# Operand loads of the output projection moved from SyncE's queue to ScalarE's, and the transposes of a token block pinned behind the next block's products

## The chip, the cores and the metric

One NeuronCore of a Trainium2 chip runs one program. The metric is the device time of one execution in microseconds (us). The engines of the core are TensorE (PE in the profile, with its weight loads as PEld), VectorE (DVE), ScalarE (ACT), GpSimd (POOL) and SyncE (SP). Each engine takes its instructions in order and waits at the head of its queue until what the instruction needs is there. A DMA is issued by an instruction in such a queue, too: by SP or by ACT here.

## The reference

Two layers of a decoder trunk over 1024 tokens of width 1024. A layer normalizes its input, projects it, runs several branches (attention of different kinds, in layer 0 a short convolution as well), gates and concatenates them to y, and adds an output projection to the residual stream:

```python
def even_layer(h, mem, layer, norm_g, w_in, w_out, ...):
    u = rms_norm(h, norm_g)
    proj = u @ w_in
    ...
    ya = differential_attention(aq, ak, av, a_qn, a_kn, a_lam, a_on, lam_init)
    yb = short_gated_conv(bh, bc, bb, b_cw, b_cb)
    yx = memory_cross_attention(xq, mem, mem_g, w_mem_kv, x_qn, x_kn)
    y = jnp.concatenate([ya * jax.nn.silu(az), yb * jax.nn.silu(bz), yx * jax.nn.silu(xz)], axis=-1)
    return h + y @ w_out

def rms_norm(x, g):
    xf = x.astype(jnp.float32)
    y = xf * lax.rsqrt(jnp.mean(xf * xf, axis=-1, keepdims=True) + EPS)
    return (y * g.astype(jnp.float32)).astype(x.dtype)
```

The odd layer ends in the same way (forgetting attention and memory attention, no convolution). y has 2048 features in both layers. The first 1024 of them in layer 0 come from differential attention, whose output is normalized per head and token; the kernel applies that factor late, as told below.

## The kernel before

Matrix products in float32 are made of three products of split operands: every operand is written as a high part (a rounded copy, made by ACT, L128) and a low part (the rest, a subtraction on DVE or POOL, L129). `split` (L125) does both.

**The output projection** (`out_proj`, L759, once per layer) multiplies y (tokens by 2048) with a weight of 2048 by 1024. y lies in DRAM, features by tokens (`y_dr`). The 1024 output columns are done in two halves. Half 0 (L773) takes the tokens in pairs of blocks of 128 and fetches and splits the second half's weights meanwhile. Half 1 (L784) takes the eight token blocks one by one, and carries the next layer's entry with it in layer 0: when a block is complete, DVE adds the residual into `hb` (L792), SP stores it (L793), `norm_rows` (L131) normalizes it (ACT's Square, two small steps on POOL, L120 and L122, and `xn` on DVE, L137), and `turn_rows` (L139) transposes `xn` on PE (eight transposes of 128 by 128, L146) and splits the result into the operands `u` of layer 1. The transposes of a block are called as `turn` in the next block's round (L791); those of the last block are kept as `turn_last` and called in layer 1's first projection unit, behind its token block 2 (L205).

`out_blocks` (L728) does the products of a block. For each quarter j of the features it loads a tile yr of 128 by 512 (L739, 256 KB, five buffers). In layer 0 and for j below 2 it also loads the norm factor rn, spread over the partitions (L742, 256 KB, four buffers), and POOL multiplies yr by it (L743). yr is split into yh2 (ACT) and yl2 (DVE), three buffers each, and 12 products follow (L750 to L752). Then the residual's tile rs is loaded (L755). In half 1 of layer 0 the left half of a block, stored before, is loaded back into hb (L788).

**What sets the order.** The kernel is written in a tile framework that schedules every engine's instructions by priorities and by dependencies; the order on an engine is fixed when it is built. All loads and stores stand in SP's queue in this kernel. A load into a buffer waits for the last reader of what was in it: a yr for the DVE split of the yr five tiles before, an rn for POOL's L743 of four tiles before, yh2 and yl2 for PE's products of three tiles before.

Of the kernel before, what the change touches and what calls it, by code (L numbers as in the profile page):

```python
# [15 lines left out]
P = 128  # L16
T = 1024
D = 1024
KC = D // P
# [14 lines left out]
class Trunk:  # L34
# [152 lines left out]
    def token_unit(self, weights, lhs_hi, lhs_lo, nblk, post, together=False):  # L187

        nc = self.nc
# [3 lines left out]
        for t0 in range(0, nblk, step):  # L193
            blks = [(tb, self.bank("pd", "ds"[tb % 2] if together or self.boot else "d"), lhs_hi(tb), lhs_lo(tb)) for tb in range(t0, t0 + step)]
            for k in range(KC):
                h, l = wh[k], wl[k]
                for tb, ps, ah, al in blks:
                    nc.tensor.matmul(ps[:, :n], lhsT=ah(k), rhs=h, start=(k == 0), stop=False)  # L198
                    nc.tensor.matmul(ps[:, :n], lhsT=ah(k), rhs=l, start=False, stop=False)  # L199
                    nc.tensor.matmul(ps[:, :n], lhsT=al(k), rhs=h, start=False, stop=(k == KC - 1))  # L200
            for tb, ps, _, _ in blks:
                with self.tc.high_priority(PRIO_EVAC):
                    post(tb, ps)
            if self.turn_last is not None and t0 == 2:
                self.turn_last()  # L205
                self.turn_last = None
            self.tick()
# [520 lines left out]
    def out_blocks(self, layer, tbs, half, tiles, res, pool, fetch=None):  # L728
# [4 lines left out]
        for j in range(4):  # L733
            if fetch is not None:
                fetch(range(4 * j, 4 * j + 4))
            for tb, ps in zip(tbs, pss):
                ts = slice(tb * P, (tb + 1) * P)
                yr = pool.tile([P, 4, P], F32, name="yr2", tag="yr", bufs=5)
                nc.sync.dma_start(out=yr, in_=self.y_dr[layer][j * 512:(j + 1) * 512, ts].rearrange("(c p) t -> p c t", p=P))  # L739
                if layer == 0 and j < 2:  # L740
                    rn = pool.tile([P, 4, P], F32, name="rn", tag="rn", bufs=4)
                    nc.sync.dma_start(out=rn, in_=self.on_dr[4 * j:4 * j + 4, ts].unsqueeze(0).broadcast_to([P, 4, P]))  # L742
                    nc.gpsimd.tensor_tensor(out=yr, in0=yr, in1=rn, op=ALU.mult)  # L743
# [3 lines left out]
                for i in range(4):  # L747
# [3 lines left out]
                    nc.tensor.matmul(ps, lhsT=yh[:, i, :], rhs=l, start=False, stop=False)  # L751
                    nc.tensor.matmul(ps, lhsT=yl[:, i, :], rhs=h, start=False, stop=(c == 15))  # L752
        for tb, ps in zip(tbs, pss):
# [5 lines left out]
    def out_proj(self, layer, w, res, dst, g_next):  # L759
        nc, tc = self.nc, self.tc  # L760
        with tc.tile_pool(name=f"p2_{layer}", bufs=1, reuse_waits="tile") as p2:
# [22 lines left out]
            for tb in range(NB):  # L784
# [5 lines left out]
                if turn is not None:  # L790
                    turn()  # L791
                nc.vector.tensor_tensor(out=hb[:, 512:], in0=ps, in1=rs, op=ALU.add)  # L792
# [92 lines left out]
```

## Time and profile before

| | us |
|---|---|
| median of 3 runs | 2289.31 (2287.74 to 2291.7) |
| profiled execution | 2293.37 |
| its span in the profile | 2291.6 |
| PE busy in the span | 2198.5 (96%) |
| ACT busy | 1060.1 (46%) |
| layer 0's output projection, about | 950 to 1183 |
| of this, half 1 | 1051 to 1183 |
| layer 1's output projection, about | 2108 to 2290 |

The profiled execution lies 1.8 us above its span, and 4.1 above the median of the runs. A time on the trace's axis counts from the start of the span. In a timeline row an entry such as "x2" means two instructions put together, with the time from the first one's start to the last one's end or the sum of their durations, and the part in brackets is the engine's idle time before it, with what released it.

### The profile page before, as it was taken

To read this page: it belongs to the slowest core of one execution; us is meant where nothing else is said; L and a number is where in the kernel's file an instruction comes from. 1 tells how busy PE (TensorE), PEld (TensorE's weight loads), DVE (VectorE), ACT (ScalarE), POOL (GpSimd) and SP (SyncE) were. 2 spreads that over 40 slices of the span, in tenths; PEclk is the share of its full clock that TensorE was granted. 3 is DMA by queue.
4 is the path that set the end of the run, shared out by engine and by line. 5 is a ranking of instruction groups with operands and counts; after the bars stand their busy time and mean duration, and the time that the engine had idled before them with its cause. 6 is when DMAs were issued, how large, how long until landed. Compare 5 with 4: busy or idle time off the path is not lost.

```text
span 2291.6 us, 35847 instructions
## 1 busy us (share of the span) xinstructions
PE 2198.5 (96%) x12528; PEld 1983.2 (87%) x12528; DVE 1241.3 (54%) x2860; ACT 1060.1 (46%) x2503; POOL 1023.6 (45%) x1356
## 2 busy tenths in 40 slices
PE   7999999999999999797889999999999999998999
PEld 7889989889889899575678999999999999996887
DVE  5646756656656665542334555555555555656332
ACT  5656455555465464421234444444444444545221
POOL 4665555555555552331135555445555555522000
PEclk9999999999999999799999999999999999999999
DMA  5450110210210221665632221121222221215543
GB/s 159 133 148 22 56 55 23 63 55 17 69 46 24 74 70 48 200 196 133 156 104 50 56 55 40 37 51 44 56 54 56 56 61 42 63 49 167 164 148 95
DMA packets 266077, 183.07 MB, mean 80 GB/s; under 512 B 24572, under 2 KB 242844, under 8 KB 265896
## 3 DMA queue, kind: packets, MB, share of 16 engines
q1 hardware_dynamic: 265896, 180.77, 27.9%
q8 instruction: 99, 1.62, 0.3%
q14 instruction: 82, 0.67, 0.1%
HBM read 153.32 MB, written 27.38 MB: 79 GB/s over the span
## 4 chain that ended last, share of the span: by engine, by line
PE 45%; DMA 4%; POOL 2%; DVE 1%; issue 1%; ACT 1%; SPq 0%; POOLq 0%; DVEq 0%; ACTq 0%
PE pd L198 6%; PE pd L200 6%; PE pd L199 6%; PE pss L390 4%; PE pd L750 3%; PE pd L752 3%; PE pd L751 3%; DMA yr<-y_dr 3%; PE pd L230 2%; PE pd L231 2%; PE pd L232 2%; PE pt L424 2%; PE po L438 1%; PE po L437 1%; PE po L436 1%; PE pt L279 1%
## 5 line engine op out<-in xcount | busy, mean ns | idle before, releaser
L198 PE MATMUL pd<-wqh,u 128*128 128x384 f32 (+2 forms) x1536 | 515.1, 337 | 0.6 <-ACT u L128 0.6
L199 PE MATMUL pd<-wql,u 128*128 128x384 f32 (+2 forms) x1536 | 514.1, 335 | 0.0
L200 PE MATMUL pd<-wqh,u 128*128 128x384 f32 (+2 forms) x1536 | 513.1, 334 | 0.0
L198 PEld LDWEIGHTS pd<-wqh,u 128*128 128x128 f32 x1536 | 291.1, 190 | 4.8 <-ACT u L128 1.1
L199 PEld LDWEIGHTS pd<-wql,u 128*128 128x128 f32 x1536 | 291.2, 190 | 4.7 <-DVE wql L129 0.2
L200 PEld LDWEIGHTS pd<-wqh,u 128*128 128x128 f32 x1536 | 290.9, 189 | 4.4
L231 PE MATMUL pd<-u,wfl 128*128 128x512 f32 x704 | 278.2, 395 | 0.8 <-POOL wfl L129 0.8
L232 PE MATMUL pd<-u,wfh 128*128 128x512 f32 x704 | 277.9, 395 | 0.0
L230 PE MATMUL pd<-u,wfh 128*128 128x512 f32 x704 | 277.7, 396 | 0.0
L129 POOL TENSOR_TENSOR wql<-raw,wqh 128x384 fp32r<-128x384 f32 (+2 forms) x220 | 219.3, 1009 | 74.8 <-ACT wqh L128 71.8
L128 ACT ACTIVATE yh<-yr 128x512 fp32r<-128x512 f32 x128 | 80.8, 632 | 277.9 <-PE pd L751 159.1
L270 DVE TENSOR_TENSOR qr<-qr,rs_r 128x256 f32<-128x256 f32 x200 | 139.1, 695 | 104.2 <-POOL rs_r L122 102.2
L129 DVE TENSOR_TENSOR yl<-yr,yh 128x512 fp32r<-128x512 f32 x128 | 95.9, 756 | 173.9 <-ACT yh L128 173.6
L128 ACT ACTIVATE pth<-pt 128x512 fp32r<-128x512 f32 (+1 forms) x232 | 122.2, 555 | 134.4 <-PE pt L424 133.0
L122 POOL TENSOR_TENSOR rs_r<-rs_v,neghalf 128x2 f32<-128x2 f32 (+2 forms) x220 | 177.7, 809 | 14.1
L686 POOL TENSOR_TENSOR fbias<-ck,cqn 128x896 f32<-128x896 f32 (+3 forms) x96 | 110.2, 1149 | 155.7 <-DVE mx L407 124.1
L128 ACT ACTIVATE wqh<-raw 128x384 fp32r<-128x384 f32 (+2 forms) x256 | 118.5, 481 | 117.5 <-DMA raw<-in_e_w_in_dram 64.8
L129 DVE TENSOR_TENSOR ptl<-pt,pth 128x512 fp32r<-128x512 f32 (+1 forms) x232 | 144.0, 640 | 44.4 <-ACT pth L128 41.8
L129 POOL TENSOR_TENSOR wfl<-rawf,wfh 128x512 fp32r<-128x512 f32 x88 | 121.0, 1377 | 100.7 <-ACT wfh L128 100.3
L129 POOL TENSOR_TENSOR vl<-qr,vh 128x128 fp32r<-128x128 f32 x160 | 80.8, 511 | 177.5 <-ACT vh L128 170.2
L231 PEld LDWEIGHTS pd<-u,wfl 128*128 128x128 f32 x704 | 132.5, 188 | 28.0 <-issue 1.4
L232 PEld LDWEIGHTS pd<-u,wfh 128*128 128x128 f32 x704 | 132.3, 188 | 27.6 <-issue 1.1
(257 smaller groups left out, 5002.0 us busy)
## 6 DMA issues: line engine op xcount, KB each, us to landing
yr<-y_dr SPq DMA_DIRECT2D x128, 256.0 KB
raw<-in_o_w_in_dram SPq DMA_DIRECT2D x288, 64.0 KB
rawf<-in_e_w_in_dram SPq DMA_DIRECT2D x56, 256.0 KB
y_dr<-y SPq DMA_DIRECT2D x112, 128.0 KB
raw<-in_e_w_in_dram SPq DMA_DIRECT2D x192, 64.0 KB
wraw<-in_e_w_out_dram SPq DMA_DIRECT2D x32, 256.0 KB
rn<-on_dr SPq DMA_DIRECT2D x32, 256.0 KB
rawf<-in_o_w_in_dram SPq DMA_DIRECT2D x32, 256.0 KB
```

The costliest lines, as they stand in the source:

```text
L122: nc.gpsimd.tensor_tensor(out=r[:, :n], in0=v[:, :n], in1=self.neghalf[:, :n], op=ALU.pow)
L128: nc.scalar.activation(out=hi, in_=src, func=AF.Copy)
L129: lo_eng.tensor_tensor(out=lo, in0=src, in1=f32(hi), op=ALU.subtract)
L198: nc.tensor.matmul(ps[:, :n], lhsT=ah(k), rhs=h, start=(k == 0), stop=False)
L199: nc.tensor.matmul(ps[:, :n], lhsT=ah(k), rhs=l, start=False, stop=False)
L200: nc.tensor.matmul(ps[:, :n], lhsT=al(k), rhs=h, start=False, stop=(k == KC - 1))
L230: nc.tensor.matmul(ps, lhsT=h, rhs=uh[:, k, :], start=(k == 0), stop=False)
L231: nc.tensor.matmul(ps, lhsT=l, rhs=uh[:, k, :], start=False, stop=False)
L232: nc.tensor.matmul(ps, lhsT=h, rhs=ul[:, k, :], start=False, stop=(k == KC - 1))
L270: nc.vector.tensor_tensor(out=v, in0=v, in1=r.unsqueeze(2).broadcast_to([P, ng, gs]), op=ALU.mult)
L390: nc.tensor.matmul(ps, lhsT=q[qb // 4][rows, qs], rhs=k[c0 // 512][rows, ks], start=(i == 0), stop=(i == n - 1))
L686: nc.gpsimd.tensor_tensor(out=b[:, :kext], in0=ck[:, :kext], in1=self.cqn[:, qb, h:h + 1].broadcast_to([P, kext]), op=ALU.subtract)
```

## The change

Two loads of `out_blocks` are issued by ScalarE in place of SyncE: yr (128 DMAs, 64 per layer) and rn (32, in layer 0 only). And two calls of `turn_rows` are put under `issue_after(...)`, which pins what is called inside behind a given instruction in the engines' order: in half 1 of layer 0's projection the transposes of block tb - 1 behind the last product of block tb, and the transposes of the last block behind the last product of token block 2 in layer 1's first unit.

```diff
@@ token_unit
-                    nc.tensor.matmul(ps[:, :n], lhsT=al(k), rhs=h, start=False, stop=(k == KC - 1))
+                    mm = nc.tensor.matmul(ps[:, :n], lhsT=al(k), rhs=h, start=False, stop=(k == KC - 1))
...
             if self.turn_last is not None and t0 == 2:
-                self.turn_last()
+                with self.tc.issue_after(mm.ins):
+                    self.turn_last()
                 self.turn_last = None
@@ out_blocks
                 yr = pool.tile([P, 4, P], F32, name="yr2", tag="yr", bufs=5)
-                nc.sync.dma_start(out=yr, in_=self.y_dr[layer][j * 512:(j + 1) * 512, ts].rearrange("(c p) t -> p c t", p=P))
+                nc.scalar.dma_start(out=yr, in_=self.y_dr[layer][j * 512:(j + 1) * 512, ts].rearrange("(c p) t -> p c t", p=P))
                 if layer == 0 and j < 2:
                     rn = pool.tile([P, 4, P], F32, name="rn", tag="rn", bufs=4)
-                    nc.sync.dma_start(out=rn, in_=self.on_dr[4 * j:4 * j + 4, ts].unsqueeze(0).broadcast_to([P, 4, P]))
+                    nc.scalar.dma_start(out=rn, in_=self.on_dr[4 * j:4 * j + 4, ts].unsqueeze(0).broadcast_to([P, 4, P]))
                     nc.gpsimd.tensor_tensor(out=yr, in0=yr, in1=rn, op=ALU.mult)
...
-                    nc.tensor.matmul(ps, lhsT=yl[:, i, :], rhs=h, start=False, stop=(c == 15))
+                    self.last_mm = nc.tensor.matmul(ps, lhsT=yl[:, i, :], rhs=h, start=False, stop=(c == 15))
@@ out_proj
                 if turn is not None:
-                    turn()
+                    with tc.issue_after(self.last_mm.ins):
+                        turn()
```

In the changed kernel the lines behind `mm = ` keep their numbers up to L203; from there they are one higher (yr is loaded at L740, rn at L743, the products are L751 to L753), and behind `turn()` two higher.

In PE's order, one block of half 1 in layer 0 before (`xn_13201` is a block's normalized rows, `yl_13274` the low part of the next block's last quarter):

```order
L146 MATMUL pt<-ident,xn_13201 128x128 x3
L752 MATMUL pd<-wo_12_11786,yl_13274 128x512
L750 MATMUL pd<-wo_13_11787,yh_13273 128x512
L751 MATMUL pd<-wo_13_11803,yh_13273 128x512
L752 MATMUL pd<-wo_13_11787,yl_13274 128x512
L750 MATMUL pd<-wo_14_11788,yh_13273 128x512
L751 MATMUL pd<-wo_14_11804,yh_13273 128x512
L752 MATMUL pd<-wo_14_11788,yl_13274 128x512
L750 MATMUL pd<-wo_15_11789,yh_13273 128x512
L751 MATMUL pd<-wo_15_11805,yh_13273 128x512
L752 MATMUL pd<-wo_15_11789,yl_13274 128x512
L146 MATMUL pt<-ident,xn_13201 128x128 x5
```

and the same place in the changed kernel:

```order
L751 MATMUL pd<-wo_14_11788,yh_13273 128x512
L752 MATMUL pd<-wo_14_11804,yh_13273 128x512
L753 MATMUL pd<-wo_14_11788,yl_13274 128x512
L751 MATMUL pd<-wo_15_11789,yh_13273 128x512
L752 MATMUL pd<-wo_15_11805,yh_13273 128x512
L753 MATMUL pd<-wo_15_11789,yl_13274 128x512
L146 MATMUL pt<-ident,xn_13201 128x128 x8
L751 MATMUL pd<-wo_0_11774,yh_13322 128x512
L752 MATMUL pd<-wo_0_11790,yh_13322 128x512
```

Three of the eight transposes stood inside the last quarter's products, ahead of the first one that reads yl; all eight now stand behind the block's last product. At the end of half 1 the order before was

```order
L752 MATMUL pd<-wo_15_11789,yl_13380 128x512
L146 MATMUL pt<-ident,xn_13307 128x128 x5
L146 MATMUL pt<-ident,xn_13413 128x128 x8
L198 MATMUL pd<-wqh,u_12583 128x396 x3
L199 MATMUL pd<-wql,u_12583 128x396
L200 MATMUL pd<-wqh,u_12585 128x396
```

and the transposes of the last block (`xn_13413`) now stand behind the 72 products of layer 1's first three token blocks:

```order
L198 MATMUL pd<-wqh,u_12583 128x396
L199 MATMUL pd<-wql,u_12583 128x396
L200 MATMUL pd<-wqh,u_12585 128x396
L146 MATMUL pt<-ident,xn_13413 128x128 x8
L280 MATMUL pt<-ident,qr 128x128
L198 MATMUL pd<-wqh,u_12583 128x396
```

SP's order of one round in half 1 before (`hb` and `rs` as above, the stores to `h_dr` are those of L793):

```order
L793 DMA h_dr_77<-hb1_11808 128x512
L755 DMA rs_13077<-in_x_dram 128x512
L739 DMA yr2_12953<-y_dr0_75 128x4x128
L788 DMA hb1_11808<-h_dr_77 128x512
L739 DMA yr2_12999<-y_dr0_75 128x4x128
L739 DMA yr2_13020<-y_dr0_75 128x4x128
L742 DMA rn_13213<-on_dr_81 128x4x128
L739 DMA yr2_13041<-y_dr0_75 128x4x128
L742 DMA rn_13234<-on_dr_81 128x4x128
L793 DMA h_dr_77<-hb0_11807 128x512
```

ACT's order of the same round in the changed kernel, with these loads among its own work:

```order
L740 DMA yr2_12953<-y_dr0_75 128x4x128
L128 ACTIVATE yh2_12849<-yr2_12847 128x512
L740 DMA yr2_12999<-y_dr0_75 128x4x128
L128 ACTIVATE yh2_12898<-yr2_12893 128x512
L740 DMA yr2_13020<-y_dr0_75 128x4x128
L128 ACTIVATE yh2_12919<-yr2_12914 128x512
L743 DMA rn_13213<-on_dr_81 128x4x128
L740 DMA yr2_13041<-y_dr0_75 128x4x128
L743 DMA rn_13234<-on_dr_81 128x4x128
L128 ACTIVATE yh2_12937<-yr2_12935 128x512
L128 ACTIVATE u00_12583<-pt_12867 128x4x128
L135 ACTIVATE xn2_12883,nb_ms_12884<-hb0_11807 128x1024
```

The loads keep their order among themselves; SP's queue keeps the stores, rs and hb, and ACT's yh, u and Square now stand between and behind loads. The orders of DVE and POOL are nearly the same in both kernels.

## Rows read from the trace of the kernel before

**Rows 1.** The page: busy time of PE, its share of the span and its instructions.

```profile
PE 2198.5 (96%) x12528; PEld 1983.2 (87%) x12528; DVE 1241.3 (54%) x2860; ACT 1060.1 (46%) x2503; POOL 1023.6 (45%) x1356
```

**Rows 2.** Windows of 20 us: start and end, length, then busy time of PE, PEld, DVE, ACT and POOL with instruction counts, PE's granted clock as a share of full speed, busy share of the DMA engines, GB/s. The first three are in layer 0's output projection, the last in layer 1's.

```profile
1020.00:1040.00 20.00, 16.65 (x67) 11.70 (x66) 4.96 (x7) 3.16 (x5) 5.07 (x4) 1.00 0.51 118
...
1140.00:1160.00 20.00, 16.25 (x70) 12.93 (x70) 6.83 (x10) 6.01 (x11) 4.37 (x5) 0.91 0.73 194
1160.00:1180.00 20.00, 20.00 (x91) 16.17 (x90) 9.60 (x13) 6.34 (x12) 3.50 (x6) 1.00 0.16 54
...
2140.00:2160.00 20.00, 20.00 (x90) 16.57 (x89) 6.04 (x9) 4.84 (x8) 0.00 (x0) 1.00 0.51 156
```

**Rows 3.** Timeline of POOL from 1020 to 1156: the first and the last of the seven pairs of L743 in half 1 that start six rounds.

```profile
1050.82 2.50 POOL L743 TENSOR_TENSOR yr<-yr,rn 128x512 f32<-128x512 f32 x2 [16.07 <-issue]
...
1149.42 2.51 POOL L743 TENSOR_TENSOR yr<-yr,rn 128x512 f32<-128x512 f32 x2 [12.83 <-DMA yr<-y_dr]
```

**Rows 4.** The chain of waits, 1150 to 1183, where PE runs without a stop: start, time, what.

```profile
1168.16 0.33 PE pt L146 x3
...
1170.82 0.55 PE pt L146 x5
...
1182.47 0.24 PE pd L751
1182.71 0.23 PE pd L752
```

**Rows 5.** The same view, 1050 to 1112: one turn of the loop in half 1.

```profile
1086.24 1.77 POOL yr L743 x2
...
1090.22 1.90 DVE yl L129 x3
...
1093.64 8.39 DMA yr<-y_dr
1102.06 1.90 POOL yr L743 x2
```

**Rows 6.** Waits of the engines, 985 to 1200: who waited for what, us in total, times, longest.

```profile
POOL yr L743 <- DMA yr<-y_dr: 113.0, 11, 17.3
...
PE pt L146 <- DVE xn L137: 20.8, 6, 6.2
```

**Rows 7.** The chain of waits again, at 1020 to 1060 and at 2098 to 2112: times of yr loads.

```profile
1035.23 6.78 DMA yr<-y_dr
...
1043.60 3.65 DMA yr<-y_dr
...
2104.18 3.12 DMA yr<-y_dr
```

**Rows 8.** Timeline of SP, 1062 to 1112: its issues in the round of rows 5, with the time that each held SP.

```profile
1087.27 0.46 SPq L739 DMA_DIRECT2D yr<-y_dr  x1
...
1090.33 1.80 SPq L788 DMA_DIRECT2D hb<-h_dr  x1
1092.22 2.21 SPq L739 DMA_DIRECT2D yr<-y_dr  x2
1102.74 0.36 SPq L742 DMA_DIRECT2D rn<-on_dr  x1
```

**Rows 9.** Waits of SP's queue, 985 to 1200, columns as in rows 6.

```profile
SPq L742 <- POOL yr L743: 56.2, 13, 8.9
SPq L755 <- DMA h_dr<-rs: 26.7, 6, 8.6
```

**Rows 10.** Instructions by line and form, 1090 to 1135: count, busy us, mean ns of one, idle before with releasers.

```profile
L129 DVE TENSOR_TENSOR yl<-yr,yh 128x512 fp32r<-128x512 f32 x12 | 7.7, 684 | 0.0
...
L137 DVE SCALAR_TENSOR_TENSOR xn<-hb,rs_r,gb 128x1024 f32<-128x1024 f32 x3 | 3.9, 1285 | 24.8 <-POOL rs_r L122 24.8
...
L128 ACT ACTIVATE u<-pt 128x512 fp32r<-128x512 f32 x6 | 3.4, 593 | 0.1
L135 ACT ACTIVATE xn<-hb 128x1024 f32<-128x1024 f32 x3 | 3.2, 1054 | 0.0
...
L135 ACT ACTIVATION_READ_ACCUMULATOR xn<-hb 128x1 f32 x3 | 0.6, 197 | 0.0
```

**Rows 11.** Timeline, 2100 to 2108: the start of layer 1's output projection (`pth` is the last attention head's).

```profile
2100.20 3.89 SPq L442 DMA_DIRECT2D y_dr<-y  x3
...
2100.54 0.60 ACT L128 ACTIVATE pth<-pt 128x512 fp32r<-128x512 f32 x1 [1.01 <-PE pt L424]
...
2104.18 2.68 SPq L739 DMA_DIRECT2D yr<-y_dr  x5
...
2107.38 0.63 ACT L128 ACTIVATE yh<-yr 128x512 fp32r<-128x512 f32 x1 [4.17 <-DMA yr<-y_dr]
```

**Rows 12.** Timelines of POOL and PE at the passage into layer 1, 1186 to 1212: the split of layer 1's first weights, the last block's transposes, the last weight tile of the first unit, and PE's next wait.

```profile
1186.14 4.96 POOL L129 TENSOR_TENSOR wql<-raw,wqh 128x396 fp32r<-128x396 f32 x4
...
1188.40 1.94 PE L146 MATMUL pt<-ident,xn 128*128 128x128 f32 x8 [4.90 <-DVE xn L137]
...
1196.74 1.04 POOL L129 TENSOR_TENSOR wql<-raw,wqh 128x396 fp32r<-128x396 f32 x1 [0.98 <-ACT wqh L128]
...
1207.67 0.30 PE L279 MATMUL pt<-ident,qr 128*128 128x128 f32 x1 [3.62 <-DVE qr L270]
```

**Rows 13.** The view by tile of yr, 1023 to 1155: duration of its issues in ns, least, median and most, first and last start.

```profile
L739 SPq DMA_DIRECT2D yr<-y_dr x35: 359/459/3903, 1023.9 to 1154.8; - x35
```

## The prediction, made before the changed kernel ran

> **What bounds the kernel now.** I read the page's busy times first: TensorE (PE) works for 96% of the span [rows 1], so of 2291.6 us only some 93 can be won, and only where PE stands idle. The windows by stage say where: in layer 0's output projection PE is busy some 16 of each 20 us, while in its last 20 us, and in layer 1's output projection once it runs, it is busy all of the time [rows 2]. The change touches the first of these, the passage from it into layer 1, and the start of the second.
>
> Inside the projection the second half of the columns runs block by block. The POOL timeline gives its beat: the pair of products yr times rn (L743) starts at 1050.82 for block 1 and at 1149.42 for block 7, six rounds in 98.6 us, 16.4 each [rows 3]. PE needs less: products follow each other some 0.235 us apart (0.23 and 0.24 by turns in the chain), 48 of them are 11.3, and a block's eight transposes 0.33 + 0.55 [rows 4], together 12.2. So PE isn't the limit there, and a round is a loop around it. The chain of waits shows that loop: POOL's pair, then yl on DVE, a late yr issue on SP behind it, 8.39 us of DMA yr, and the next pair [rows 5]. The waits agree: POOL waited 113 us for yr [rows 6]. That DMA time is a queue's and not the transfer's own: a yr that was issued with little before it landed in 3.65 us, one 8 us earlier in 6.78 [rows 7].
>
> Why the issue is late is in SP's rows. The last two yr of a round start at 1092.22, behind a reload of hb that takes 1.80 to issue, and then SP stands until 1102.74, when an rn may go because POOL has freed its buffer [rows 8]. SP waited 56.2 us for POOL's L743 and 26.7 for the stores of rs [rows 9]: one in-order queue carries yr, rn, rs, hb and both stores, and whichever is not ready holds the rest.
>
> **The change, part by part.** Let T be the end of POOL's pair (1088.01 in the chain: 1086.24 + 1.77). Before, the deciding yr is the second of the two whose issue SP begins at T + 4.2 (1092.22, [rows 8]); its transfer counts from T + 5.6 (1093.64), lands at T + 14.0 (1102.03), and the next pair ends at T + 15.9 [rows 5].
>
> 1. The yr and rn issues move to ScalarE (ACT). In its order of a round, after T: rn 0.4, yh 0.63, u 0.59, the Square 1.05 + 0.20, u 0.59, yr 0.4, yh 0.63, which is 4.5; the 0.4 is SP's usual issue [rows 8], yh is in [rows 11], and the others are ACT's own [rows 10]. Beside them rs_v and rs_r (0.9) follow the Square's end at 2.9, so DVE's xn, with a u of DVE's own ahead of it, starts at some T + 4.2 and ends at 5.5, and the yl behind it at 6.15 (0.68) [rows 10]. That frees the buffer of the first yr of the next block: issue to 6.6, yh to 7.25, yl to 7.9, and the second yr is issued at T + 7.95. That is later than before, since ACT now stands in the loop with its own work. But nothing of SP's stands ahead of it: at 3.65 to land [rows 7], 0.1 to be released, and 1.27 for its L743 (half of a pair, [rows 3]), the next pair ends at T + 13.0. With 3.12, the shortest landing that I found [rows 7], it is 12.4; PE's own 12.2 is the floor; with 6.78 it would be 16.1. I take 13.0: six rounds are 78.0 against 98.6, **-20.6**. Ends: -25.4 at PE's need, -2.0 at 6.78.
>
> What waits behind: rn on ACT waits for the L743 of four tiles earlier, and behind it in ACT's order stand yh, both u and the Square. POOL waits for all of these. In the round above that is counted, since T is just that release; what it takes away is ACT's lead, for before its yh stood ahead of T wherever PE had freed their buffers.
>
> 2. The end. From the end of block 7's pair (1151.93) to the last product (1182.94) there are 31.0 us [rows 3, 4]; with 48 products a block that is two and a half blocks at PE's rate, so little is to be had: PE's wait for xn at the first transposes, and a stretch at the lower clock (0.91 over 1140 to 1160, [rows 2]). **-2**, ends 0 and -4.
>
> 3. The first half of the columns has the same queue. PE lacks 3.35 of 20 us at 1020 to 1040 [rows 2], and the first half goes on to 1050 at that rate, which makes 5. **-3**, ends 0 and -5.
>
> 4. The transposes by themselves. Before, three of the eight stood ahead of the last chunk's yl products and five behind them; PE waited 20.8 us for xn there, in six waits [rows 6]. It looks like the prize, and I price it at nothing of its own: the product behind the transposes needs a yl that stands behind the same xn in DVE's order, so PE would wait there for yl instead. It is counted within the 13.0.
>
> 5. The junction. Before, the last block's eight transposes wait 4.90 us for xn until 1188.40, and layer 1's first products stand behind them. The products of three token blocks end at 1204.05 (1207.67 less the 3.62 that PE then waits for qr) [rows 12]. Now these 72 products come first, and their operands are there earlier: the first four wql are split on POOL from 1186.14 to 1191.10. The products can run in step with the wql tiles, whose last ends at 1197.78 [rows 12]; with nine products behind it, at up to 0.27 each (PE took 13.7 us over the 72 before, 0.19 each, and some of these may fall at the lower clock), they end at 1199.4 to 1200.2 in place of 1204.05. The transposes (1.94) fall into the wait for qr. **-3.9**, ends 0 (if qr comes no earlier) and -4.9.
>
> 6. Layer 1 starts its projection earlier. SP issues the first yr at 2104.18 behind three stores of y that take it 3.89, and PE starts behind its yh, 2107.38 + 0.63 [rows 11]. ACT is past its last pth at 2101.14 and issues yr there [rows 11]. That is 3.0 at most; the five issues (2.68 on SP) now stand ahead of ACT's splits of wo, which takes a little back: **-2.5**, ends 0 and -3. After 2120 PE is full [rows 2], so the other loads there bring nothing.
>
> 7. Layer 0's start. The same first nine issues that SP makes there in a burst stand on ACT ahead of its first yh, and PE waits for yh either way. **0**; by one dear issue more or less, at the longest of yr's (3.90, [rows 13]), ends -3.9 and +3.9.
>
> Sum: 20.6 + 2 + 3 + 3.9 + 2.5 = 32.0 less than the profiled 2293.37, 2261.4. The profile was 4.06 above the median of the runs, 2289.31, so I forecast 2257.
>
> The Trainium skill speaks against part 1: "DMA: Bandwidth & Descriptors", section "Issuing engines are not separate DMA queues", has transfers run on the same DMA engines whichever engine starts them, and a second issuer save only issue time. The rows show both: the engines are half busy here (0.51 to 0.73, [rows 2]), and landing times go from 3.65 to 8.39. By that rule alone the landing would stay, which is the first rival; the same page's "Queues, rings and completion order" has a DMA engine take packets from its queues in turn, by which a yr on ACT's queue needn't wait for all of SP's, and the sum above holds.
>
> **Rivals.** *Shared engines.* Four yr and two rn of 256 KB and SP's rs, hb and stores are the same bytes as before; if the DMA engines' backlog, and not SP's order, sets the landing, the deciding yr lands at T + 14.0 as now, and the next pair ends at T + 15.3. Six rounds are 91.8, -6.8; with 1 each for parts 2 and 3, the 3.9 of the junction and 1.5 in layer 1, -14.2: 2275. For it: a DMA share of 0.73 in 1140 to 1160 [rows 2]; against it: SP issues nothing for 8 us of each round [rows 8] and shares of 0.5 leave half.
>
> *Other side: ACT pays the burst price.* An issue takes 0.36 to 0.46 at most times, but the rows also have 1.80 and 3.90 [rows 8, 13]. On SP that delays loads alone. On ACT it holds yh, u and the Square. Four issues stand in the loop; at the hb's 1.80 each they add 4 x 1.40 = 5.6 to the 13.0, 18.6 a round: +13.2, the junction -3.9, and the rest nothing: 2299. It decides from a round of 17.05 (3.9 / 6 over 16.4), a mean issue of 1.4 us on ACT. Against it: the median of yr's 35 issues is 0.459 [rows 13].
>
> *It moves, and the loop stays.* Rn's wait for POOL goes with it to ACT, and yh behind it. If the gain from the queue is eaten by that, rounds stay at 16.4, and only the junction is left: 2285, no change that could be told.
>
> **How the numbers follow.** Forecast 0.56, its own range 2243 (25.4 + 4 + 5 + 4.9 + 3 + 3.9 less) to 2266 (a landing of 5 us); shared engines 0.26, 2266 to 2281; no change 0.10; ACT's burst price 0.08. The first two hold 0.82, so the range is 2243 to 2281. A measurement of this kernel can tell 0.2%, 4.6 us: faster 0.82, the same 0.10, slower 0.08.
>
> **What would show it.** Right: L743 pairs 12.4 to 14 us apart; yr landing in 3 to 5 us; SP's wait for L743 gone; transposes with no wait for xn; the first product of layer 1 some 3 to 4 us behind the last wo product; layer 1's first yr within 1 us of pth. Wrong: pairs 15 apart with landings of 8 us (shared engines); issues on ACT over 1 us and ACT's idle time put down to its own queue (burst price); PE's wait for xn merely renamed to yl at the same length (no change).

## The result, and the profile after

| | before | after |
|---|---|---|
| median of the runs, us | 2288.52 (2287.27 to 2291.7, 4 runs) | 2267.81 (2264.08 to 2269.93, 4 runs) |
| profiled execution, us | 2293.37 | 2269.93 |
| its span | 2291.6 | 2267.9 |

The changed kernel takes 0.9906 of the time of the kernel before, with a 95% interval of 0.9888 to 0.9923: 20.7 us less between the medians, 23.7 between the two spans. The forecast was 2257 us in a range of 2243 to 2281. The time lies in the range, somewhat more than half way from the forecast to the first rival's 2275, and 1.8 us above 2266, the upper end of the forecast's own range: it falls into the stretch that the prediction gave to shared engines.

The same points of the program, taken from the timelines and the views by line of the two profiles, say where it went. A stage runs from one point to the next, and each point is the start of the instruction named; times are in us.

| stage | before | after | difference |
|---|---|---|---|
| A: start of the last pth of layer 0's attention, to the first product of its output projection | 12.9 | 15.1 | +2.2 |
| B: to the last product of half 0 | 100.3 | 102.6 | +2.3 |
| C: to the last product of half 1 | 131.4 | 106.8 | -24.6 |
| D: to the first transpose of qr in layer 1 (L279, now L280) | 25.2 | 22.5 | -2.7 |
| E: to the last pth of layer 1's attention | 892.9 | 893.5 | +0.6 |
| F: to the first product of layer 1's output projection | 7.6 | 3.7 | -3.9 |
| G: to its last product | 179.3 | 181.1 | +1.8 |

The seven sum to -24.3; the rest is 0.6 more ahead of A. Stage E, which the change does not touch, lies between 891.8 and 893.5 in all profiles but two (895.3 and 896.6), and B was 100.3, 102.7 and 101.2 in three profiles of kernels with the same half 0. So a difference of 2 us in one stage of one profile tells little, and those in A and B are read from groups of runs below.

The page of the changed kernel has PE at 7 us less of busy time, and a second queue:

```profile
PE 2191.5 (97%) x12528; PEld 1976.6 (87%) x12528; DVE 1242.9 (55%) x2860; ACT 1059.4 (47%) x2503; POOL 1022.4 (45%) x1356
...
q1 hardware_dynamic: 181416, 138.82, 21.3%
q10 hardware_dynamic: 84480, 41.95, 7.0%
```

q10 is ACT's queue: 41.95 MB, the 160 loads of 256 KB. ACT's busy time is what it was, since issues do not count as busy. PE's 7 us lie in half 1. Half 1 by windows, columns as in [rows 2], before and now:

```profile
1051.10:1182.50 131.40, 107.45 (x436) 82.88 (x435) 43.60 (x60) 33.57 (x58) 25.86 (x30) 0.92 0.48 128
...
1056.20:1163.00 106.80, 99.53 (x433) 77.55 (x432) 42.11 (x58) 32.28 (x57) 23.98 (x28) 0.98 0.55 147
```

Of the 24.6 us, PE's idle time gave 16.7 (24.0 before, 7.3 now) and its busy time 7.9, at a granted clock of 0.98 in place of 0.92, a mean of stretches at full speed (2.4 GHz) and at half of it (1.2 GHz). The prediction counted no clock in the loop, and here it need not have: before, the chain of waits from 1050.82 to 1154.35 has no product in it, so slower products did not set the six rounds.

**The loop in half 1.** Timeline of POOL, the L744 pairs (L743 before) that answer to [rows 3]:

```profile
1045.44 2.54 POOL L744 TENSOR_TENSOR yr<-yr,rn 128x512 f32<-128x512 f32 x2 [12.64 <-issue]
...
1130.07 1.30 POOL L744 TENSOR_TENSOR yr<-yr,rn 128x512 f32<-128x512 f32 x1 [7.70 <-DMA yr<-y_dr]
...
1139.76 3.31 POOL L744 TENSOR_TENSOR yr<-yr,rn 128x512 f32<-128x512 f32 x2 [5.33 <-DMA yr<-y_dr]
```

Eight pairs belong to half 1, blocks 0 to 7. The timeline that the prediction was made from ended at 1156 and so left out the eighth pair of the kernel before, 9.5 us behind the last one of [rows 3]:

```profile
1158.92 3.00 POOL L743 TENSOR_TENSOR yr<-yr,rn 128x512 f32<-128x512 f32 x2 [6.04 <-DMA yr<-y_dr]
```

What [rows 3] calls the pairs of blocks 1 and 7 in the prediction are those of blocks 0 and 6. The six rounds between them are the same six in both kernels: 98.6 us before, 84.6 now (1045.44 to 1130.07), 14.1 a round. The six do not gain alike. In the kernel before, the second round was the long one, 19.8 us:

```profile
1065.73 2.50 POOL L743 TENSOR_TENSOR yr<-yr,rn 128x512 f32<-128x512 f32 x2 [12.41 <-DMA yr<-y_dr]
1085.53 2.48 POOL L743 TENSOR_TENSOR yr<-yr,rn 128x512 f32<-128x512 f32 x2 [17.29 <-DMA yr<-y_dr]
```

Its chain of waits is not the loop of [rows 5]; SP holds a load of rs until a store of the earlier rs has landed, and then once more:

```profile
1067.48 10.21 DMA h_dr<-rs
...
1078.15 3.34 DMA h_dr<-rs
```

This round takes 14.2 now and gives 5.6 of the 14.0 us. The first gives 2.2, the other four, which were turns of the loop of [rows 5], 0.9 to 2.5 each (15.6 to 16.3 before, 13.8 to 15.2 now). From block 6's pair to the last product it is 33 us in both (1149.42 to 1182.5, 1130.07 to 1163.0). What else half 1 won lies at its front: block 0's pair now starts 10.8 us ahead of half 0's last product (1056.2), where before it started with it (1050.82 against 1051.1). Half 0 itself ends later now: from the last pth to block 0's pair it is 112.9 us before and 106.9 now, so 6.0 of the 10.5 are a pair that comes earlier, and 4.5 are what half 0 lost.

The chain of waits of one round, to be laid beside [rows 5]:

```profile
1068.41 4.70 DMA yr<-y_dr
...
1082.93 4.81 DMA yr<-y_dr
...
1087.77 1.91 POOL yr L744 x2
...
1089.70 0.37 ACTq L743
...
1090.12 0.64 ACT yh L128
...
1094.60 0.69 DVE yl L129
...
1095.31 0.37 ACTq L740
...
1095.72 0.64 ACT yh L128
...
1096.39 0.71 DVE yl L129
...
1097.12 5.85 DMA yr<-y_dr
...
1102.99 1.85 POOL yr L744 x2
...
1112.27 4.66 DMA yr<-y_dr
```

Here T is 1089.68. The rn that waited for L744 goes, and yh behind it; the yl behind xn ends at T + 5.6, the second yr is issued at T + 7.44, lands at T + 13.3, and the next pair ends at T + 15.2. Three other rounds of this view have 4.70, 4.81 and 4.66 of DMA in that place. The loop of [rows 5] is there still, on another engine: ACT's own queue is the link.

**The start of the projection.** ACT's timeline behind the last pth:

```profile
938.52 0.38 ACTq L740 DMA_DIRECT2D yr<-y_dr  x1
...
940.66 0.52 ACTq L740 DMA_DIRECT2D yr<-y_dr  x1
946.12 0.37 ACTq L743 DMA_DIRECT2D rn<-on_dr  x1
...
950.89 0.63 ACT L128 ACTIVATE wo<-wraw 128x512 fp32r<-128x512 f32 x1 [11.77 <-DMA rn<-on_dr]
...
952.98 0.61 ACT L128 ACTIVATE yh<-yr 128x512 fp32r<-128x512 f32 x1
```

and the chain of waits at the same place:

```profile
940.20 5.90 DMA y_dr<-y
...
946.12 5.95 DMA rn<-on_dr
```

Nine loads stand in ACT's order ahead of four splits of wo and of the first yh. After five, ACT stands until 946.12, when a store of y (issued by SP, and of no concern to this rn) has landed. Two more of the nine are held: an rn until 949.18 by another store of y, a yr until 950.47 by SP's load of gb. POOL's first product with rn was done at 945.85 (944.59 and 1.26), but its yh came at 952.98.

**The junction and layer 1.** Timelines of PE at the junction and of ACT at the start of layer 1's projection, to be laid beside [rows 12, 11]:

```profile
1166.51 0.81 PE L198 MATMUL pd<-wqh,u 128*128 128x396 f32 x3 [2.19 <-ACT wqh L128]
...
1181.74 1.03 PE L146 MATMUL pt<-ident,xn 128*128 128x128 f32 x8
...
1185.46 0.45 PE L280 MATMUL pt<-ident,qr 128*128 128x128 f32 x1 [2.68 <-DVE qr L271]
```

```profile
2078.99 2.65 ACTq L740 DMA_DIRECT2D yr<-y_dr  x5
...
2082.04 0.63 ACT L128 ACTIVATE yh<-yr 128x512 fp32r<-128x512 f32 x1 [2.48 <-DMA yr<-y_dr]
```

The last block's transposes show no wait any more, and the first yr of layer 1 leaves as the last pth starts.

### The profile page after: what moved, and what is told of

It reads as the page before. It is cut to its first block, busy times and chain, and to the rows that moved or that the text cites. A ratio compares the mean times of both kernels' runs of the same rounds, so it can differ in the third digit from the quotient of the medians.

```text
span 2267.9 us, 35860 instructions
## 1 busy us (share of the span) xinstructions
PE 2191.5 (97%) x12528; PEld 1976.6 (87%) x12528; DVE 1242.9 (55%) x2860; ACT 1059.4 (47%) x2503; POOL 1022.4 (45%) x1356
## 3 DMA queue, kind: packets, MB, share of 16 engines
q10 hardware_dynamic: 84480, 41.95, 7.0%
## 4 chain that ended last, share of the span: by engine, by line
PE 83%; DMA 7%; DVE 3%; POOL 2%; ACT 2%; issue 2%; ACTq 0%; SPq 0%; POOLq 0%; DVEq 0%
PE pd L199 11%; PE pd L200 11%; PE pd L198 11%; PE pss L391 7%; PE pd L231 7%; PE pd L232 7%; PE pd L233 7%; PE pt L425 4%; PE pd L753 3%; PE pd L751 3%; PE pd L752 3%; DMA yr<-y_dr 2%; PE po L439 2%; PE po L438 2%; PE po L437 2%
## 5 line engine op out<-in xcount | busy, mean ns | idle before, releaser
L122 POOL TENSOR_TENSOR rs_r<-rs_v,neghalf 128x2 f32<-128x2 f32 (+2 forms) x220 | 178.1, 810 | 14.1
L129 POOL TENSOR_TENSOR wfl<-rawf,wfh 128x512 fp32r<-128x512 f32 x88 | 119.8, 1363 | 101.2 <-ACT wfh L128 101.0
```

Of the source, the lines that this page charges most:

```text
L122: nc.gpsimd.tensor_tensor(out=r[:, :n], in0=v[:, :n], in1=self.neghalf[:, :n], op=ALU.pow)
L129: lo_eng.tensor_tensor(out=lo, in0=src, in1=f32(hi), op=ALU.subtract)
```

## The experiments

All times are medians of runs beside runs of the kernel before on the same chip; ratios are to these, with a 95% interval. The table gives the stages of each profile as above (A + B from the last pth to the end of half 0, since both hang on the loads there), the six rounds of L743 or L744 as a mean, and the medians. extra_load has its eight loads in A and B, as told below.

| run | A + B | C | D | F | G | round | median, us | ratio |
|---|---|---|---|---|---|---|---|---|
| before | 113.2 | 131.4 | 25.2 | 7.6 | 179.3 | 16.4 | 2288.52 | |
| after | 117.7 | 106.8 | 22.5 | 3.7 | 181.1 | 14.1 | 2267.81 | 0.9906 (0.9888 to 0.9923) |
| queue_only | 118.2 | 106.1 | 26.3 | 3.8 | 181.0 | 13.9 | 2274.13 | 0.9938 (0.9916 to 0.9960) |
| pins_only | 115.7 | 128.3 | 22.2 | 7.4 | 178.7 | 15.8 | 2284.97 | 0.9992 (0.9980 to 1.0003) |
| half1_act | 122.8 | 107.4 | 21.5 | 3.8 | 180.4 | | 2269.03 | 0.9921 (0.9896 to 0.9946) |
| first_j0_act | 119.5 | 106.9 | 21.6 | 3.8 | 178.4 | | 2266.55 | 0.9909 (0.9882 to 0.9936) |
| first_pair_sp | 118.0 | 106.9 | 22.6 | 3.7 | 180.3 | | 2267.51 | 0.9912 (0.9896 to 0.9929) |
| rn_sp | 107.9 | 102.8 | 22.7 | 3.8 | 184.0 | 13.5 | 2258.59 | 0.9871 (0.9856 to 0.9886) |
| rn_pool | 121.3 | 121.4 | 22.5 | 3.7 | 179.6 | | 2284.65 | 0.9987 (0.9978 to 0.9997) |
| yr_sp | 125.9 | 111.2 | 22.6 | 7.7 | 179.5 | 14.9 | 2283.89 | 0.9973 (0.9961 to 0.9985) |
| extra_load | 120.6 | 107.4 | 22.6 | 3.8 | 180.1 | 14.1 | 2267.40 | 0.9909 (0.9894 to 0.9924) |
| rn_sp_last | 108.4 | 103.8 | 22.2 | 3.7 | 183.2 | | 2260.62 | 0.9880 (0.9865 to 0.9895) |
| rn_sp_yr6 | 110.8 | 104.1 | 21.6 | 3.7 | 184.2 | | 2261.73 | 0.9883 (0.9861 to 0.9904) |
| layer1_act | 114.2 | 126.7 | 21.4 | 3.7 | 180.6 | | 2281.55 | 0.9970 (0.9960 to 0.9980) |

### Queue or pins

**queue_only** takes the pins out of the changed kernel:

```diff
-                with self.tc.issue_after(mm.ins):
-                    self.turn_last()
+                self.turn_last()
...
-                    with tc.issue_after(self.last_mm.ins):
-                        turn()
+                    turn()
```

> Only the two loads move to ACT's queue; no transposes are pinned (they stand 3 + 5 in PE's order, and the last block's ahead of layer 1's first products, as before). My theory (the queue makes the loop, the pins only the junction): L743 pairs 13.5 to 14 us apart in half 1, half 1 some 107 to 109 us long, the junction's 2.6 us not won: 2270 to 2272 us. Rival (the transposes' wait for xn was what cost the time, and the pins are the prize): rounds stay at 15.5 or more, half 1 at 120 or more, 2280 or more.

**pins_only** takes the queue change out:

```diff
-                nc.scalar.dma_start(out=yr, ...
+                nc.sync.dma_start(out=yr, ...
-                    nc.scalar.dma_start(out=rn, ...
+                    nc.sync.dma_start(out=rn, ...
```

> Only the transposes are pinned; all loads stay on SP's queue. My theory: rounds stay at 16.4, half 1 at 131, PE's wait for xn becomes a wait for yl of the same length; the junction alone is 2.6 shorter: 2286 us. Rival (the pins are the prize): half 1 falls to 110 or less, 2268 or less.

With the queue alone half 1 is as short as in the changed kernel (106.1), and the time 2274.1, some 2 us over what was expected. With the pins alone half 1 is 128.3, and 2285.0 cannot be told from the kernel before. So the queue carries the gain, and the pins are worth the junction's 2.5 to 4.9 us (D: 25.2 and 26.3 without, 21.4 to 22.7 with them in all runs). The medians of the changed kernel and of queue_only lie 6.3 apart: D has 3.8 of that, and stage E, 896.6 in queue_only's profile, 3.1; that this 3.1 comes from the pins was not shown, for the kernel before has 892.9 without them. What became of PE's wait for xn [rows 6] shows in the waits of pins_only:

```profile
POOL yr L744 <- DMA yr<-y_dr: 108.7, 11, 15.4
...
PE pd L753 <- DVE yl L129: 19.8, 8, 7.4
```

PE waited 20.8 us for xn before; now it waits 19.8 for yl, behind the same xn in DVE's order, and POOL waits nearly as long as before for yr (113.0 in [rows 6]). The wait that looked like the prize has changed its name. Half 1 is 3.1 us shorter in this profile all the same (4.7 in that of layer1_act, with the same loads in layer 0), and A + B is 2.5 longer; the medians show no more than the junction's 3.

**rn_sp_last** tests the seven pins once more, where the queue's wait is smaller (its base is rn_sp, told below):

```diff
-                    with tc.issue_after(self.last_mm.ins):
-                        turn()
+                    turn()
```

> As the run with yr on ACT and rn on SP, but only the last block's transposes are pinned; the other seven blocks' stand 3 + 5 as before. My theory (the seven pins are worth nothing of their own): half 1 within 1.5 us of 102.8, 2257 to 2261 us. Rival (with the queue's wait gone, PE's wait for xn shows): half 1 at 106 to 112, 2263 to 2268.

C is 103.8 against 102.8, and 2260.6 us against 2258.6, with intervals that overlap for the most part. The seven pins are worth some 2 us at most, and nothing that these runs resolve.

### The start and half 0

**half1_act** leaves half 0 of layer 0 on SP, **first_j0_act** only a part of its first two blocks, **first_pair_sp** its first two blocks:

```diff
             for tb, ps in zip(tbs, pss):
+                q = nc.scalar if layer == 1 or half == 1 else nc.sync
...
-                nc.scalar.dma_start(out=yr, ...
+                q.dma_start(out=yr, ...
-                    nc.scalar.dma_start(out=rn, ...
+                    q.dma_start(out=rn, ...
```

with `layer == 1 or half == 1 or tb > 1 or j == 0` in the second and `layer == 1 or half == 1 or tb > 1` in the third.

> As the changed kernel, but in layer 0's half 0 the loads stay on SP. My theory: the 4.5 us that the profile shows lost between the last pth and half 1's start come from nine loads that stand in ACT's order ahead of its splits of wo and its first yh, one of them held 5.9 us by a store of y; with SP's queue there the first product comes 13 us behind the last pth as before and half 1 is as short as in the changed kernel: 2263 us. Rival (half 0 needs the queue as well, the 5 us come from elsewhere, such as more transfers at once): 2267 to 2270.

> As the changed kernel, but of layer 0's first two blocks in half 0 only the first quarter's yr and rn (four loads) are on ACT, the other three quarters' on SP. My theory: none of the four waits for a store, so the splits of wo and the first yh aren't held, and the first product comes 4 to 8 us earlier than in the changed kernel: 2259 to 2263 us. Rival (the burst's landing, not ACT's order, sets the start): as half1_act or no better than 2266.

> As the changed kernel, but the first two blocks of half 0 in layer 0 are loaded by SP, all later ones by ACT. My theory: the start (from the last pth to the first product) is 12.9 us as before and not 15.1, and the rest of half 0 is as in the changed kernel, 92 us behind the first product on a u tile: 2263 to 2265 us. Rival (SP's weights for half 0 then stand behind loads again, as in the run with the first quarter alone on ACT): half 0 ends no earlier than in the changed kernel, 2267 to 2270.

A is 12.9, 11.8 and 12.6 where the changed kernel has 15.1 and queue_only 14.6 (extra_load, with the same loads ahead of yh, 13.6). So the nine loads ahead of ACT's yh cost the start some 1 to 2 us. In first_j0_act that is 3.3 and not the 4 to 8 expected, and its premise was wrong, that none of its four loads waits for a store: the fourth, an rn, left at 946.46, as a store of y issued at 941.20 had landed. And my theory of the whole fell: none of the three is faster than the changed kernel, and what the start won went in half 0. In half1_act the chain shows how, in two rows:

```profile
1008.79 5.77 DMA h_dr<-rs
...
1018.86 3.79 DMA yr<-y_dr
```

SP held a load of rs until a store of the earlier rs had landed, then once more, and the yr behind it left at 1018.86. It is the wait that [rows 9] has for L755. Where loads of half 0 stay on SP, they stand behind its stores and its weights; where they go to ACT, yh stands behind them. Over the kernels with both loads on ACT throughout (after, queue_only) A + B is 118.0 on the mean, over those with all of layer 0 on SP (before, pins_only, layer1_act) 114.4.

### Which of the two loads

**rn_sp** has only yr on ACT, **yr_sp** only rn, **rn_pool** yr on ACT and rn on POOL:

```diff
 rn_sp
-                    nc.scalar.dma_start(out=rn, ...
+                    nc.sync.dma_start(out=rn, ...
 yr_sp
-                nc.scalar.dma_start(out=yr, ...
+                nc.sync.dma_start(out=yr, ...
 rn_pool
-                    nc.scalar.dma_start(out=rn, ...
+                    nc.gpsimd.dma_start(out=rn, ...
```

> As the changed kernel, but rn is loaded by SP again; only yr is on ACT. My theory (in the changed kernel ACT's rn, which waits for L743, holds yh, u and the Square behind it, so that the loop runs through ACT's whole round): without that wait ACT runs ahead of POOL's pair, the deciding yr is issued by the pair's end, rounds fall to PE's need of 12.2 to 12.6 and half 1 to 98 to 101 us; the start has five loads fewer ahead of ACT's first yh: 2256 to 2261 us. Rival (the loop is set by the landing time of yr behind other transfers, 4.7 to 5.9 us now): rounds stay at 13.2 to 13.8, half 1 at 105 or more, 2265 to 2268. Second rival (rn comes late behind SP's stores): rounds of 14.5 or more, 2272.

> As the changed kernel, but yr is loaded by SP again; only rn is on ACT. My theory (yr must leave SP's queue, and rn must not enter ACT's): it has the worse half of both, yr behind SP's hb and rs, and yh behind rn's wait on ACT: half 1 at 122 to 132 us, of the gains the junction alone, 2280 to 2288. Rival (what had to leave SP was rn, whose wait for L743 held yr there for 56 us): with rn gone SP's yr run free, half 1 at 103 to 110, 2260 to 2268.

> As the changed kernel, but rn is loaded by POOL, whose L743 is what frees its buffer. My theory: as for rn on SP, ACT isn't held, rounds of 12.2 to 12.8; POOL pays some time for each issue (unknown here, bounds 0.4 to 2 us, two a round, beside its idle time of 8 us a round): 2256 to 2262 us. Rival (landing sets the loop): 2265 to 2268.

rn_sp takes 2258.6 us, 0.9871 of the time before, and is the fastest kernel of this study: better than the change as made by 9 us, and inside what my theory expected. Its mechanism was only half right, though. Rounds did not fall to 12.2 to 12.6; they are 13.5, and half 1 is 102.8. (The expectation's 13.2 to 13.8 counted seven rounds, the last and shortest one too; so counted it is 12.8 here and 13.5 in the changed kernel.) The chain of waits shows what took the gain back:

```profile
1069.99 7.33 DMA yr<-y_dr
1077.35 1.87 POOL yr L744 x2
...
1084.01 7.73 DMA yr<-y_dr
```

With T at 1079.22, the deciding yr leaves at T + 4.8 in place of T + 7.4, as the theory had it; but it takes 7.73 to land where the changed kernel has 4.7 to 5.9, and lands only 0.8 us sooner, at T + 12.5. That is the side of the rival.

The larger part of the gain over the changed kernel lies in A + B, 107.9 against 117.7; half 1 has 4.0. There, too, ACT's order had rn (waiting for POOL's product four tiles earlier) ahead of yh; without it PE has no idle time at all from 1000 to 1050. The first of the five windows of 10 us of rn_sp, columns as in [rows 2]:

```profile
1000.00:1010.00 10.00, 10.00 (x45) 8.29 (x45) 4.20 (x7) 2.54 (x4) 2.60 (x2) 1.00 0.81 200
```

The changed kernel's 20 us there:

```profile
1000.00:1020.00 20.00, 17.09 (x72) 13.28 (x73) 5.92 (x9) 3.80 (x6) 3.60 (x4) 1.00 0.66 184
```

Some of it is given back: G, layer 1's projection, is 183 to 184 us in rn_sp and in the two runs made from it, against 181.1 and less elsewhere, though the kernel's lines for layer 1 are those of the changed kernel. The timeline has PE waiting there for yh and yl behind splits of wo whose weights have not landed; I didn't try to mend that.

yr_sp's time came out as I expected (2283.9), and again not its parts. Half 1 is 111.2, between my 122 to 132 and the rival's 103 to 110: what rn does on SP was by itself much of what kept half 1 long, and taking either load off SP shortens it by 17 (rn) or 25 us (yr), from the 128.3 of pins_only. The time is lost in A + B, 125.9.

rn_pool refutes its expectation. POOL's timeline shows where the time goes:

```profile
1079.83 0.79 POOL L743 DMA_DIRECT2D rn<-on_dr  x1 [4.05 <-issue]
1080.63 1.27 POOL L744 TENSOR_TENSOR yr<-yr,rn 128x512 f32<-128x512 f32 x1
1085.37 0.77 POOL L743 DMA_DIRECT2D rn<-on_dr  x1 [3.46 <-issue]
```

Each rn on POOL shows 0.8 us, and ahead of 13 of half 1's 16 stand 3.1 to 5.0 in which POOL waits for nothing that the profile shows (ahead of the other three, 0.4). What POOL does in it was not shown; read as the price of the issue, it is some 5 us, and where my bounds of 0.4 to 2 us would have left a round room, this does not. Half 1 is 121.4. Only the start is short: A is 6.9, with no rn in ACT's way and one wait of 1.7 us for a store.

### What sets the landing

**extra_load** has one more load in the source of each of half 1's rounds in layer 0, into a tile that nothing reads:

```diff
-            p2.tile([P, 784], F32, name="gap")
+            gap = p2.tile([P, 784], F32, name="gap")
...
+                if layer == 0:
+                    nc.sync.dma_start(out=gap[:, :512], in_=w[tb * P:(tb + 1) * P, 512:])
                 ((ps, rs),) = self.out_blocks(layer, [tb], 1, w1, res, p2)
```

> As the changed kernel, with one more load of 256 KB in each of half 1's eight rounds in layer 0, on SP's queue, into a tile that nothing reads. Theory 1 (what is left of a round over PE's need is ACT's own order; the DMA engines have room): rounds within 0.3 us of 13.5, half 1 within 3 us of 106.8: 2266 to 2271 us. Theory 2 (the DMA engines' common bandwidth sets yr's landing): 256 KB at the 150 to 190 GB/s that move in half 1 are 1.4 to 1.7 us, all of it in the loop: half 1 at 116 to 120, 2278 to 2281 us.

The time is that of the changed kernel, 2267.4 us. But the run does not test what it was made for. The view by tile of gap has all eight loads ahead of half 1, which begins at 1056.1 in this profile:

```profile
L791 SPq DMA_DIRECT2D gap<-in_e_w_out_dram x8: 327/376/1273, 939.6 to 998.7; - x8
```

Nothing reads the tile and w is there from the start, and the framework's order has them in A and B. Half 1 (107.4, rounds of 14.1) had no byte more than before, and neither theory is decided. What is on record on the landing of the deciding yr is from the other runs: 8.1 to 10.0 us in the kernel before (the rounds from 1093.64 on), 4.7 to 5.9 in the changed kernel, where the DMA engines moved more in a microsecond (147 against 128 GB/s in half 1), and 6.9 to 7.7 in three rounds of rn_sp, where it leaves sooner (5.2 in a later one). The bytes of a round alone don't set it, for they are the same in all three. How much of it is due to other transfers under way stays open.

**rn_sp_yr6** takes rn_sp and gives yr a sixth buffer:

```diff
-                yr = pool.tile([P, 4, P], F32, name="yr2", tag="yr", bufs=5)
+                yr = pool.tile([P, 4, P], F32, name="yr2", tag="yr", bufs=6)
...
-            p2.tile([P, 784], F32, name="gap")
```

> As the run with yr on ACT and rn on SP, with six buffers of yr in place of five (the pad tile of half 1 left out). Theory 1 (what is left of half 1 over PE's need of 96.6 is a yr issue that waits for the split five tiles before, and then lands 7 us later): a load goes one tile earlier, half 1 falls from 102.8 to 97 to 100, 2253 to 2256 us. Theory 2 (it is ACT's order, or landing that stretches with whatever is issued together): half 1 stays at 102 to 104, 2257 to 2261.

Half 1 stays at 104.1, and 2261.7 us is no better than with five. Its chain shows what takes the buffer's place:

```profile
1066.25 6.28 DMA rn<-on_dr
...
1072.60 7.66 DMA yr<-y_dr
```

ACT's yr leaves when an rn has landed that SP issued, and that this yr has nothing to do with. It is the same kind of wait as that of ACT's rn for a store of y at the start. The order of the built program names it; these are rows of the changed kernel's ACT queue at the start, with what they wait for:

```
L740 DMA yr2_11866<-y_dr0_75 128x4x128 [waits DMAHW0_49]
L743 DMA rn_11868<-on_dr_81 128x4x128 [waits DMAHW1_49]
L740 DMA yr2_11887<-y_dr0_75 128x4x128 [waits DMAHW2_49]
```

Each DMA of either queue takes the next of eight completion semaphores (DMAHW0 to DMAHW7) and first waits for the DMA that had it before. The rn in the second row is the one that left at 946.12, and in rn_sp_yr6 the rn of 1066.25 and the yr of 1072.60 have one semaphore. So the two queues stay tied: a load on ACT can wait for a store on SP. That this is all that is left in half 1 was not shown; it was not tried with more semaphores.

### Layer 1 alone

**layer1_act** has the pins, and yr on ACT in layer 1 only (`q = nc.scalar if layer == 1 else nc.sync` in the diff above).

> Pins, and yr on ACT in layer 1 alone; layer 0 loads all by SP. My theory: layer 0 as in the run with pins alone (half 1 at 128 us), and from the last pth to layer 1's first product 3.7 us in place of 7.4 to 7.6: 2280 to 2282 us. Rival (the gain there is given back within layer 1's projection): 2284 to 2286.

It is 2281.6 us, 3.4 less than pins_only, and F is 3.7 against 7.4: as expected. G is 180.6 against 178.7, so of F's 3.7 some 2 are given back in this profile.

## Why the prediction was right, and where it was wrong

The direction, the step that carries it (the loads' order in SP's queue held half 1 long) and the range held. The forecast was 10.8 us too low, and the time lies above its own range of 2243 to 2266. Its sum was put together from parts of which two were mis-sized and one had the wrong sign, and a gain that it did not have, at the front of half 1, made up for much of that: so far the nearness of the total is luck. By its steps:

1. *The loop moves to ACT, and a round is 13.0 us.* In the turn shown, the order of events was right nearly to the instruction: yl was to end at T + 6.15 and did at T + 5.6, the second yr to be issued at T + 7.95 and was at T + 7.44. Two of its numbers were too small: the landing, taken at 3.65 from a load with little before it, is 4.7 to 5.9 in this loop; and L744 counts 1.85 and not 1.27, because the pair's first product is still running when the second yr lands. Six rounds are 84.6 us in place of 78.0: 14.0 of the 20.6 us. And the turn that it took for all six was four of them; 5.6 of the 14.0 come from the one round that stood behind the stores of rs. The step that was mis-sized is the landing: 3.65 was measured on one load at another place, and in rn_sp, where the yr leaves 2.6 us sooner, it is 6.9 to 7.7. Why is open.

2. *The end, -2.* It is 0: 33 us from block 6's pair to the last product, before and now. I had named the pair wrongly, from a timeline that ended too early. What the sum lacked is the front of half 1: the freed queue brings block 0's operands 10.8 us ahead of half 0's last product, and about 10.5 of C's 24.6 are from there. The slips cancel by luck: parts 1 and 2 together were 22.6, and C is 24.6.

3. *Half 0 wins 3*, and 7, *the start is nothing*. This is where the forecast failed: A + B is 4.5 longer, in place of 3 shorter. Part 7 said that "PE waits for yh either way", and overlooked that yh itself stands behind nine issues, of which three wait for stores and a load of SP's; its end of +3.9 has room for A's 2.2, but for another reason, one dear issue. Part 3 gave half 0 the gain of the loop and not its price. rn_sp has the price: with rn off ACT, A + B is 10 us shorter. The warning stood in the prediction, that yh, u and the Square stand behind rn's wait for L743; it was counted in half 1 only. Taken together with the front of half 1, the stretch from the last pth to block 0's pair is 6.0 shorter, where parts 3 and 7 had 3.

4. *The transposes are worth nothing of their own.* Right: pins_only has 19.8 us of waits for yl in place of 20.8 for xn, and rn_sp_last is within 2 us of rn_sp.

5. *The junction, -3.9.* It is -2.7 in the changed kernel, and -2.5 to -4.9 between runs with and without the pins. The products start where they were expected to, behind the splits of their weights (1166.51, 3 us behind the last wo product).

6. *Layer 1, -2.5.* F is 3.9 shorter, since the first yr leaves as pth starts and not as it ends; 1 to 2 us come back in G (180.2 on the mean of the eight kernels with yr on ACT there, rn_sp and the two made from it left out, and 179.2 of the three with yr on SP). The net was right.

Of the rivals, *shared engines* was not refuted. Its sign, landings of 8 us, is not there (4.7 to 5.9), but the pair of the turn shown ends at T + 15.2, where it had T + 15.3, and the mean round of 14.1 lies half way between 13.0 and 15.3. That a yr which leaves sooner takes longer to land in rn_sp speaks for it; no run tests it. *Burst price*: yr issues in the loop take 0.37 us on ACT, one of the cheapest rows of all (a single one took 3.78, at 960.48 in half 0); what holds ACT is what an issue waits for, not its own length. *It moves, and the loop stays* was true in shape and not in size.

By the rule of the Trainium skill's "DMA: Bandwidth & Descriptors", section "Issuing engines are not separate DMA queues", a second issuer saves only the time of the issues. The runs differ from it: most issues took 0.4 us on either engine, and half 1 became 25 us shorter with the queue alone (queue_only), because what SP's head waited for no longer held these loads.

## What to carry to other kernels

When a load is moved to another engine's queue, ask for each of them what it waits for before it can be issued, and what stands behind it there: in this kernel a load whose buffer that engine's own chain frees (yr, freed by the yl behind ACT's yh) gained on a compute engine's queue, and one that waits for a third engine (rn, freed by POOL) did better on SP, even among its stores. A wait that an instruction shows in the profile is a gain only if the instruction behind it has no second reason to wait at the same place; look up what that one needs, in the order of the engine that makes it. Read a timeline past the last event that a count rests on. And look up in the trace when an added load was issued, before its run is read as a test.

## What the runs showed of the hardware and the program that I had not expected

- DMAs of two queues wait for each other through the completion semaphores that the program takes in turn: ACT's rn for SP's store of y (5.90 us, at 946.12), ACT's yr for SP's rn (6.28 us, at 1072.6 in rn_sp_yr6).
- Ahead of 13 of the 16 loads that POOL issued for half 1 in rn_pool, POOL stood 3.1 to 5.0 us without a wait that the profile shows, beside 0.8 as an instruction. That this is the price of such an issue is the nearest reading, and not shown.
- The landing time of the same load of 256 KB changes with the order of issues: 3.65 and 6.78 in [rows 7], 8.1 to 10.0 in half 1 before, 4.7 to 5.9 with both loads on ACT, 6.9 to 7.7 in three rounds with yr alone there.
- TensorE's granted clock was 0.92 of full speed over half 1 before, with 24.0 us of idle time in 131.4, and 0.98 now, with 7.3 in 106.8.
